# First tile's output projection: four row blocks per PSUM chain instead of two, with its weights and half of its operands in other buffer rings

## The chip, the core and the metric

The kernel runs on one core of one Trainium2 chip. The metric is the time of one execution on the device in microseconds (us); lower is better. The engines are TensorE (PE; its weight loads are PEld), VectorE (DVE), ScalarE (ACT), GpSimd (POOL) and the queues that issue transfers, SyncE's (SP) above all. Each engine executes its own instructions in the order in which the built program has them, and waits on semaphores for the others.

## What is computed

One decoder layer over 2048 tokens of width 1024, in float32. Attention and a convolution branch are put side by side and go through one output projection; a SwiGLU network follows. Cut to what the change touches:

```python
hn = rms_norm(h, mix_pre_g)
proj = hn @ w_in                                     # A
attn_out = sliding_window_attention(q, k, v, ...)    # B, 512 columns
conv_out = conformer_conv(u, ...)                    # C, 512 columns; @ w_conv_pw at its end
mixed = jnp.concatenate([attn_out, conv_out], axis=-1) @ w_out   # W: 1024 x 1024
h = h + rms_norm(mixed, mix_post_g)                  # W's tail
hn = rms_norm(h, ffn_pre_g)
ff = (jax.nn.silu(hn @ w_gate) * (hn @ w_up)) @ w_down           # F and G
```

## The kernel before

**Tiles and stages.** The 2048 tokens are four tiles of 512. A letter and a tile number name a stage; the names in the profile carry the letter (`mm@W` is a PSUM bank written by W). A is the input projection, B attention in four blocks of 128 tokens, C the convolution with its normalization, U a product of `w_conv_pw` and half of `w_out` made once (`fold`), W the output projection, H the operands of the feed-forward part, F and G that part. A matrix operand is split in two parts (high by ScalarE, the rest by VectorE), and each product of two split operands is three matmuls of 128x512.

**W, the output projection.** Per tile it sums eight input row blocks of 128 (four from attention, four from the convolution) into four 128x1024 accumulators, `acc`, in SBUF (tag `x` for tile 0). `stage_w` goes through the row blocks in groups of `G`; for a group and a half n of the output columns it loads and splits `G` weight tiles (`weights`) and calls `block_half`: for each of the four accumulators one PSUM chain of 3 x `G` matmuls, which is then copied to `acc` by ScalarE (first group) or added to it by VectorE (the others). `acts` loads the `G` operand blocks from `mixT` by way of `wx` and splits them. For tile 0, `htags` has four entries, so `G` is 2.

**Buffers.** `t_` takes a buffer of a ring by its tag; a request waits until one is free, and requests for one tag are served in the order of the program's priorities:

```python
BUFS = dict(x=4, p=4, wx=1, gb=2, hl=8, ql=4, chl=5, mid=4, mb=2, fa=4, at=2, fc=3, glu=2, yt=1, raw=2, w=6)
mm = lambda: bank("mm", 4)
```
`raw` holds weights as they come from memory, two tiles in one buffer, for A and for W alike; `w` holds split weights, before also for both. The one `yt` buffer holds the convolution's tile (`turns[t]`, made in `stage_taps`) from the first finished channel block until `conv_tail` has normalized it and written it to `mixT`. One of the two `mb` buffers holds attention's bias. `chl` is free during the last A stage.

**Order.** The main program runs the stages A0 to A3 with `run`; the others are generators in lanes that are advanced by what the main one yields, and each `yield` says how much work was laid down. `lw` holds W0; it may start when A3 has begun, conv tile 0 is done and U is done, and W0 is finished by `lw.until("W0")` before W1. A scheduler then fixes the order of every engine from these priorities and from what each instruction waits for. The taps of the convolution (lane `lc`) have a lower priority and are tied to the pace of the products. So A3, W0, attention B2, the taps of conv tiles 1 and 2 and the tail of conv tile 1 share the engines at the same time, about 330 to 440 us into the span.

Of the kernel before, what the change touches and what calls it, by code (L numbers as in the profile page):

```python
# [13 lines left out]
F32R = mybir.dt.float32r  # L14
# [11 lines left out]
P = 128  # L26
T = 512
# [10 lines left out]
def layer_kernel(ctx, tc, x, xT, cols, rows, sinks, relb, onehot, w_in, w_pw, w_out, w_gate, w_up, w_down, out):  # L38
# [10 lines left out]
    def nm(s):  # L49
        uid[0] += 1  # L50
        return f"{s}@{lab[0]}_{uid[0]}"
# [3 lines left out]
    def t_(tag, shape, dt=F32):  # L55
        return sb.tile(list(shape), dt, tag=tag, name=nm(tag), bufs=BUFS[tag])

    def f4(tag, shape=(P, D)):
        return t_(tag, shape)
# [4 lines left out]
    def hl(tag):  # L64
        return t_(tag, (P, 2, T), F32R)
# [5 lines left out]
    def bank(tag, bufs):  # L71
        return ps.tile([P, T], F32, tag=tag, name=nm(tag), bufs=bufs)

    mm = lambda: bank("mm", 4)
# [7 lines left out]
    made = {"rows": [], "at": 0, "new": True}  # L82
# [40 lines left out]
    def split_w(raw, tag, low=None, made=False, on_pool=True):  # L123
        w = tag if not isinstance(tag, str) else hl(tag)
        if made:
            nc.sync.dma_start(w[:, 1].bitcast(F32), low)
        act(w[:, 0], raw, AF.Copy)  # L127
        if not made:
            (ptt if on_pool else vtt)(w[:, 1], raw, w[:, 0].bitcast(F32), ALU.subtract)
            if low is not None:  # L130
                nc.sync.dma_start(low, w[:, 1].bitcast(F32))
        return w

    def weight(src, low, made, raw=None, on_pool=True):
        if raw is None:
            raw = t_("raw", (P, 2, T))
            nc.sync.dma_start(raw, src)
        return [split_w(raw[:, n], "w", low[n], made, on_pool) for n in range(2)]

    def kweight(u, made, raw=None):  # L140
        hs = weight(w_in[u].rearrange("p (a b) -> p a b", a=2), lo_in[u], made, raw, u < TAPS0)
# [49 lines left out]
    def three(o, pairs, first=True, last=True):  # L191
        n = 3 * len(pairs)
        i = 0
        for (sh, sl), (mh, ml) in pairs:
            for a, b in ((sh, mh), (sh, ml), (sl, mh)):
                mat(o, a, b, start=first and i == 0, stop=last and i == n - 1)
                i += 1

    lo_in = dr.tile([2 * KC - 2, 2, P, T], F32, name="lo_in")
    lo_out = dr.tile([2, KC // 2, P, T], F32, name="lo_out")  # L200
# [54 lines left out]
    started = set()  # L255
# [461 lines left out]
    def ss(s):  # L717
        return slice((s % 4) * P, (s % 4 + 1) * P)

    def block_half(acc, units, n, first, L, bank_of, s0=0):  # L720
        cs = slice(n * T, (n + 1) * T)
        for i in range(len(acc)):
            s = i + s0
            lab[0] = L
            o = bank_of()
            three(o, [((a[s // 4][:, 0, ss(s)], a[s // 4][:, 1, ss(s)]), (w[:, 0], w[:, 1])) for a, w in units])
            if first:
                act(acc[i][:, cs], o, AF.Copy)
            else:
                vtt(acc[i][:, cs], acc[i][:, cs], o, ALU.add)  # L730
            yield 0.65 * len(units)

    def stage_w(w, atag, htags, rtags, bank_of, norm=None, ready=None):
        G = KC // len(htags)
        L = f"W{w}"
        lab[0] = L
        acc = [f4(atag) for _ in range(4)]

        def acts(gi):
            aa = []  # L740
            lab[0] = L
            n = 4 if rtags[gi] == "yt" else 2
            for c in range(G * gi, G * gi + G, n):
                ms = t_(rtags[gi][c // 2 % 2] if isinstance(rtags[gi], tuple) else rtags[gi], (P, n, T))
                nc.sync.dma_start(ms, mixT[c : c + n, :, w * T : (w + 1) * T].rearrange("c p t -> p c t"))
                for j in range(n):
                    a = hl(htags[gi])
                    act(a[:, 0], ms[:, j], AF.Copy)
                    vtt(a[:, 1], ms[:, j], a[:, 0].bitcast(F32), ALU.subtract)
                    aa.append([a])  # L750
            return aa

        def weights(gi, n):
            ws = []
            for c in range(G * gi, G * gi + G, 2):
                if c < 4:
                    ws += weight(w_out[c : c + 2, :, n * T : (n + 1) * T].rearrange("c p t -> p c t"), lo_out[n, c : c + 2], w > 0, on_pool=False)
                else:
                    for j in range(2):
                        ws.append(hl("w"))  # L760
                        nc.sync.dma_start(ws[-1].bitcast(F32), fold[n, c - 4 + j])
            return ws

        nxt = acts(0)
        yield W_LEAD
        for gi in range(KC // G):
            aa = nxt
            for n in range(2):
                lab[0] = L
                if n == 1 and gi + 1 < KC // G and not (ready and G * gi + G == 4):  # L770
                    nxt = acts(gi + 1)
                ws = weights(gi, n)
                yield from block_half(acc, list(zip(aa, ws)), n, gi == 0, L, bank_of)
            if ready and G * gi + G == 4:
                for i, c in enumerate(ready()):
                    if i == Q0 // 2:
                        ld.until("C1")
                        lh.until("B21.0")
                        lab[0] = L
                        nxt = acts(gi + 1)  # L780
                    yield c
        tail = norm_w(w, acc)
        if norm:
            norm(tail)
        else:
            yield from tail

    def norm_w(w, acc):
        L = f"W{w}"
        lab[0] = L  # L790

        def whole(src):
            t = f4("chl")
            nc.sync.dma_start(t, src)
            return t

        gb = whole(rows[0].partition_broadcast(P))
        ssq = sm(4)
        for s in range(4):
            act(junk, acc[s], AF.Square, accum_out=ssq[:, s : s + 1])  # L800
            yield 0.75
            lab[0] = L
        r = rsqrt(ssq, 4, D, w < 3)
        xs = [whole(x[w * T + s * P : w * T + (s + 1) * P]) for s in range(4)]
        ssq2 = sm(4)
        yield 3
        for s in range(4):
            lab[0] = L
            stt(acc[s], acc[s], r[:, s : s + 1], gb, ALU.mult, ALU.mult)
            yield 1.25  # L810
            lab[0] = L
            vtt(acc[s], xs[s], acc[s], ALU.add)
            r0 = w * T + s * P
            nc.sync.dma_start(h_scr[r0 : r0 + P], acc[s])
            act(junk, acc[s], AF.Square, accum_out=ssq2[:, s : s + 1])
            yield 1.25
        lab[0] = L
        r2 = rsqrt(ssq2, 4, D, w < 3)
        yield 3
        for s in range(4):  # L820
            lab[0] = L
            act(xs[s], acc[s], AF.Copy, scale=r2[:, s : s + 1])
            yield 1.25
        if w == 0:
            normed.extend(xs)
        elif w == 2:
            for k in range(KC):
                u = turn_row(w, xs, k, f2("gb"))
                nc.scalar.dma_start(hT[1][k], u)
                yield 2.0  # L830
        else:
            for k in range(4):
                t = t_("mid", (P, 2, T))
                for j in range(2):
                    turn_row(w, xs, k + 4 * j, t[:, j])
                    yield 2.0
                normed.append(t)
# [540 lines left out]
    W_LEAD = 4.0  # L1378
# [12 lines left out]
    lw = Lane(RW0, 0)  # L1391
# [3 lines left out]
    lu = Lane(0.6, 0)  # L1395
    ld = Lane(2.0, 0)
# [16 lines left out]

    lb.add("X", stage_x(), lambda: "x1" in started)
    lu.add("U", stage_fold(), lambda: "A2" in started)
    lw.add("W0", stage_w(0, "x", ["hl"] * 4, ["wx"] * 4, mm), lambda: "A3" in started and "C0" in ld.done and "U" in lu.done)
    TGA = [["hl"] * 8, ["mid"] * 4 + ["chl"] * 4, ["hl"] * 8, ["mid"] * 4 + ["hl"] * 4]
    xa = {}
    warm = mm()
# [45 lines left out]
    ws, ops = (0, 1), {}  # L1465
    for n, off in (("B11", 0), ("B21", 4)):
        lh.add(n + ".0", stage_h_plain(ws, ops, n, off))
    run(stage_w(1, "mid", ["hl", "chl"], [("wx", "mb"), "yt"], mm, norm=lambda g: lh.add("N1", g), ready=lambda: stage_pre(ws, ops, mids[0], keeps[0], 0, Q0)))
    lc.hold = lambda: "S0" not in lh.done
    lh.until("B21.0")  # L1470
# [9 lines left out]
    ws, ops = (2, 3), {}  # L1480
    lw.add("C2", stage_tail(2))
    lw.add("W2", stage_w(2, "mid", ["ql", "chl"], ["chl", "yt"], tr))
    lw.add("C3", stage_tail(3), lambda: since(lc, "T3", CS))
    lw.add("W3", stage_w(3, "mid", ["ql", "chl"], ["chl", "yt"], tr, norm=lambda g: lw.add("N3", g)))
# [73 lines left out]
```

## Time and profile before

| | |
|---|---|
| median of 3 runs | 1941.39 us (1934.53 to 1942.58) |
| profiled execution | 1939.15 us |
| its span, first to last instruction | 1937.4 us |
| granted TensorE clock, mean | 0.996 |
| busy, share of the span | PE 98%, PEld 79%, DVE 76%, ACT 50%, POOL 16% |

In the profile's rows `out<-in` names what an instruction writes and reads, x and a number is a count of instructions, then busy us and mean ns; a bracket shows how long the engine had been idle before the row, and what ended that. A row by stretches gives busy us and count for PE, PEld, DVE, ACT and POOL, then the granted clock, the share of the transfer engines and GB/s; engines with nothing in the stretch are left out. In the times of a run in order (timeline), the first number is the start, the second the duration of the merged row.

### The profile page before, as it was taken

To read this page: it belongs to the slowest core of one execution; us is meant where nothing else is said; L and a number is where in the kernel's file an instruction comes from. 1 tells how busy PE (TensorE), PEld (TensorE's weight loads), DVE (VectorE), ACT (ScalarE), POOL (GpSimd) and SP (SyncE) were. 2 spreads that over 40 slices of the span, in tenths; PEclk is the share of its full clock that TensorE was granted. 3 is DMA by queue.
4 is the path that set the end of the run, shared out by engine and by line. 5 is a ranking of instruction groups with operands and counts; after the bars stand their busy time and mean duration, and the time that the engine had idled before them with its cause. 6 is when DMAs were issued, how large, how long until landed. Compare 5 with 4: busy or idle time off the path is not lost.

```text
span 1937.4 us, 26679 instructions
## 1 busy us (share of the span) xinstructions
PE 1897.0 (98%) x8730; PEld 1532.9 (79%) x8730; DVE 1475.7 (76%) x2648; ACT 959.2 (50%) x1886; POOL 310.2 (16%) x451
## 2 busy tenths in 40 slices
PE   8999999999999999999999999999999999999997
PEld 6777777677777888787888788888788888888886
DVE  4999979995986997888669964678777766455557
ACT  5365465446748533333454555567534333345453
POOL 4010121011120011211000110002033333211003
PEclk9999999999999999999999999999999999999998
DMA  8787766657758667777577875769745443375663
GB/s 306 244 307 232 229 200 237 212 192 226 255 190 308 232 231 259 250 262 239 172 256 245 305 270 196 247 232 361 262 153 167 153 147 114 115 262 187 201 202 138
DMA packets 208556, 435.68 MB, mean 225 GB/s; under 512 B 21753, under 2 KB 39329, under 8 KB 208417
## 3 DMA queue, kind: packets, MB, share of 16 engines
q1 hardware_dynamic: 188192, 394.13, 60.8%
q0 software_dynamic: 9472, 31.46, 4.7%
q10 hardware_dynamic: 10752, 8.39, 1.3%
q8 instruction: 68, 1.11, 0.2%
q14 instruction: 72, 0.58, 0.1%
HBM read 323.26 MB, written 110.63 MB: 224 GB/s over the span
## 4 chain that ended last, share of the span: by engine, by line
PE 66%; DVE 15%; DMA 12%; issue 3%; ACT 2%; POOL 2%; SPq 0%; DVEq 0%; ACTq 0%; POOLq 0%
PE mm@F L85 30%; PE mm@G L85 17%; PE mm@A L85 8%; DVE fc@C L94 5%; PE mm@W L85 4%; PE tr@W L85 3%; PE tr@B L85 2%; DMA mids<-fa@F 2%; DMA chl@H<-hT 1%; DMA fc@G<-w_down 1%; DMA raw@A<-w_in 1%; DVE w@F L94 1%; DVE fa@F L94 1%; DVE chl@F L94 1%; DMA mixT<-yt@C 1%
## 5 line engine op out<-in xcount | busy, mean ns | idle before, releaser
L94 DVE SCALAR_TENSOR_TENSOR fc@C<-glu@C,colt,fc@C 128x512 f32<-128x512 f32 x480 | 361.2, 768 | 2.7
L85 PE MATMUL mm@F<-hl@H,w@F 128*128 128x512 f32 x1056 | 256.8, 393 | 7.2 <-ACT w@F L850 4.0
L85 PEld LDWEIGHTS mm@F<-hl@H,w@F 128*128 128x128 f32 x1056 | 198.0, 189 | 52.6 <-ACT w@F L850 5.3
L85 PE MATMUL mm@G<-hl@G,hl@G 128*128 128x512 f32 x924 | 227.5, 393 | 2.2 <-DVE hl@G L94 2.2
L850 ACT ACTIVATE w@F<-chl@F 128x512 fp32r<-128x512 f32 x220 | 135.7, 626 | 175.9 <-PE mm@F L85 144.6
L85 PE MATMUL mm@A<-hl@A,w@A 128*128 128x512 f32 x840 | 209.2, 397 | 5.1 <-ACT w@A L127 2.8
L85 PEld LDWEIGHTS mm@G<-hl@G,hl@G 128*128 128x128 f32 x924 | 171.5, 188 | 38.9 <-DVE hl@G L94 3.3
L85 PE MATMUL mm@G<-w@G,hl@G 128*128 128x512 f32 x876 | 199.4, 389 | 0.0
L85 PEld LDWEIGHTS mm@A<-hl@A,w@A 128*128 128x128 f32 x840 | 156.1, 189 | 44.7 <-issue 3.9
L85 PEld LDWEIGHTS mm@G<-w@G,hl@G 128*128 128x128 f32 x876 | 164.4, 188 | 34.1
L94 DVE TENSOR_TENSOR w@F<-chl@F,w@F 128x512 fp32r<-128x512 f32 x198 | 152.9, 777 | 46.2 <-ACT w@F L850 46.0
L85 PE MATMUL mm@F<-mid@H,w@F 128*128 128x512 f32 x528 | 132.1, 390 | 1.0 <-DVE fa@F L94 0.5
L85 PE MATMUL mm@F<-ql@H,w@F 128*128 128x512 f32 x528 | 130.0, 390 | 0.0
L85 PE MATMUL mm@F<-p@H,w@F 128*128 128x512 f32 x528 | 129.1, 389 | 0.0
L85 PE MATMUL mm@F<-x@H,w@F 128*128 128x512 f32 x528 | 125.9, 391 | 0.0
L85 PEld LDWEIGHTS mm@F<-mid@H,w@F 128*128 128x128 f32 x528 | 99.0, 188 | 22.3 <-DVE fa@F L94 1.0
L85 PEld LDWEIGHTS mm@F<-x@H,w@F 128*128 128x128 f32 x528 | 98.7, 188 | 21.3 <-issue 0.8
L85 PEld LDWEIGHTS mm@F<-p@H,w@F 128*128 128x128 f32 x528 | 99.1, 188 | 20.6
L85 PEld LDWEIGHTS mm@F<-ql@H,w@F 128*128 128x128 f32 x528 | 98.8, 188 | 20.2
L516 POOL TENSOR_SCALAR_AFFINE_SELECT p@B<-p@B 128x512 f32<-128x512 f32 x62 | 56.1, 911 | 339.6 <-ACT p@B L514 338.0
L127 ACT ACTIVATE w@A<-raw@A 128x512 fp32r<-128x512 f32 x110 | 67.4, 626 | 85.5 <-PE mm@A L85 53.2
L94 DVE TENSOR_TENSOR w@G<-raw@G,w@G 128x512 fp32r<-128x512 f32 x73 | 53.4, 731 | 71.4 <-ACT w@G L850 70.5
(320 smaller groups left out, 3253.3 us busy)
## 6 DMA issues: line engine op xcount, KB each, us to landing
mids<-fa@F SPq DMA_DIRECT2D x154, 256.0 KB, 2.9
raw@A<-w_in SPq DMA_DIRECT2D x55, 512.0 KB, 4.6
w@A<-lo_in SPq DMA_DIRECT2D x84, 256.0 KB, 3.7
fc@G<-mids SPq DMA_DIRECT2D x77, 256.0 KB, 3.3
fa@G<-mids SPq DMA_DIRECT2D x75, 256.0 KB, 4.5
w@W<-fold SPq DMA_DIRECT2D x32, 512.0 KB, 5.7
gb@F<-keeps SPq DMA_DIRECT2D x54, 256.0 KB, 3.9
chl@F<-w_gate SPq DMA_DIRECT2D x22, 512.0 KB, 5.1
```

Source lines behind the costliest of these rows:

```text
L85: r = nc.tensor.matmul(*args, **kw)
L94: r = op(*args, **kw)
L127: act(w[:, 0], raw, AF.Copy)
L516: cut = nc.gpsimd.affine_select(out=pg[:, kb].rearrange("p (i q) -> p i q", q=P), in_=pg[:, 1].rearrange("p (i q) -> p i q", q=P), compare ...
L850: act(w[:, 0], x, AF.Copy)
```

## The change

It concerns W of tile 0 alone. Its eight row blocks are taken in two groups of four, not four of two. A chain then has 12 matmuls on four row blocks, and each accumulator half is evicted twice and not four times: 8 copies by ScalarE as before, 8 additions by VectorE and not 24. Its weight tiles come from ring `chl`, not `w`. The four operands of the second group come from `yt` (one buffer for two), `mb` and `chl`. And W0 yields `W_LEAD` (4.0) ahead of each `block_half`.

```diff
-    def weight(src, low, made, raw=None, on_pool=True):
+    def weight(src, low, made, raw=None, on_pool=True, tag="w"):
...
-        return [split_w(raw[:, n], "w", low[n], made, on_pool) for n in range(2)]
+        return [split_w(raw[:, n], tag, low[n], made, on_pool) for n in range(2)]
...
-    def stage_w(w, atag, htags, rtags, bank_of, norm=None, ready=None):
+    def stage_w(w, atag, htags, rtags, bank_of, norm=None, ready=None, wtag="w"):
...
+        spare = []
+
+        def room(tag, i):
+            tag = tag if isinstance(tag, str) else tag[i]
+            if tag != "yt":
+                return hl(tag)
+            if not spare:
+                spare.append(t_("yt", (P, 2, 2, T), F32R))
+            return spare[0][:, i % 2]
...
-                    a = hl(htags[gi])
+                    a = room(htags[gi], len(aa))
...
-                    ws += weight(w_out[...], lo_out[n, c : c + 2], w > 0, on_pool=False)
+                    ws += weight(w_out[...], lo_out[n, c : c + 2], w > 0, on_pool=False, tag=wtag)
...
-                        ws.append(hl("w"))
+                        ws.append(hl(wtag))
...
+                if w == 0:
+                    yield W_LEAD
                 yield from block_half(acc, list(zip(aa, ws)), n, gi == 0, L, bank_of)
...
-    lw.add("W0", stage_w(0, "x", ["hl"] * 4, ["wx"] * 4, mm), lambda: ...)
+    lw.add("W0", stage_w(0, "x", ["hl", ["yt", "yt", "mb", "chl"]], [("wx", "wx")] * 2, mm, wtag="chl"), lambda: ...)
```

What the built program makes of it, at three places. First TensorE, ahead of the sixth product bank of A3 (`mm@A_624`). Before, these rows stand there (`tr@B_588` is a transpose in attention B2's second block):

```order
L85 MATMUL mm@W_620_3874<-w@W_616_3846,hl@W_593_3706 128x512
L85 MATMUL mm@W_617_3850<-w@W_615_3842,hl@W_592_3703 128x512 x2
L85 MATMUL mm@W_617_3850<-w@W_616_3846,hl@W_593_3706 128x512 x3
L513 MATMUL tr@B_588_3674<-ident,p@B_527_3353 128x128 x4
L85 MATMUL mm@A_624_3890<-mid@A_500_3193,w@A_622_3884 128x512 x3
```
Now these (`tr@B_689` is the last bank of B2's last block, `ct@C_576` to `ct@C_582` are the transposes at the end of conv tile 1):

```order
L513 MATMUL tr@B_686_4288<-ident,p@B_655_4090 128x128 x4
L513 MATMUL tr@B_688_4298<-ident,p@B_655_4090 128x128 x4
L85 MATMUL tr@B_689_4306<-p@B_687_4297,vtok 64x512
L85 MATMUL tr@B_689_4306<-p@B_685_4287,vtok 64x512
L85 MATMUL tr@B_689_4306<-p@B_687_4297,vtok 64x512
L85 MATMUL tr@B_689_4306<-p@B_685_4287,vtok 64x512
L640 MATMUL ct@C_576_3589<-ident,yt@C_359_2283 128x128 x4
L640 MATMUL ct@C_578_3599<-ident,yt@C_359_2283 128x128 x4
L640 MATMUL ct@C_580_3609<-ident,yt@C_359_2283 128x128 x4
L640 MATMUL ct@C_582_3619<-ident,yt@C_359_2283 128x128 x4
L85 MATMUL mm@A_624_3875<-mid@A_500_3193,w@A_622_3869 128x512 x3
```
Between the last matmul of W0's fourth chain and `mm@A_624` there are now 89 rows, all of them of attention B2 and conv tile 1: all that was left of both. Before, A3's and W0's products lay among them.

Second, VectorE: after the change the rows behind the normalization of conv tile 1 (`yt@C_359`) are W0's operands and the four weight tiles of its second block half:

```order
L94 SCALAR_TENSOR_TENSOR yt@C_359_2283<-fc@C_583_3624,yt@C_359_2283 128x4x128
L94 TENSOR_TENSOR yt@W_611_3834<-wx@W_610_3832,yt@W_611_3834 128x512 x2
L94 TENSOR_TENSOR mb@W_613_3841<-wx@W_612_3839,mb@W_613_3841 128x512
L94 TENSOR_TENSOR chl@W_614_3844<-wx@W_612_3839,chl@W_614_3844 128x512
L94 TENSOR_TENSOR chl@W_616_3849<-raw@W_615_3847,chl@W_616_3849 128x512
L94 TENSOR_TENSOR chl@W_617_3853<-raw@W_615_3847,chl@W_617_3853 128x512
L94 TENSOR_TENSOR chl@W_619_3859<-raw@W_618_3857,chl@W_619_3859 128x512
L94 TENSOR_TENSOR chl@W_620_3863<-raw@W_618_3857,chl@W_620_3863 128x512
```
Before, the splits of W0's third and fourth weight tile stood among the taps of conv tile 1, some 200 rows ahead of that point.

Third, SyncE's queue, which loads A3's sixth weights (`raw@A_621`). Before:

```order
L137 DMA raw@W_614_3840<-w_out 128x2x512
L745 DMA mb@W_762_4732<-mixT 128x2x512
L126 DMA w@A_601_3745<-lo_in 128x512
L126 DMA w@A_602_3748<-lo_in 128x512
L569 DMA glu@C_468_2961<-glu_scr 128x542
L137 DMA raw@A_621_3882<-w_in 128x1024
```
Now (`raw@W_615` and `raw@W_618` were issued some 15 rows earlier):

```order
L647 DMA mixT<-yt@C_359_2283 128x4x128 x4
L755 DMA wx@W_612_3839<-mixT 128x2x512
L755 DMA wx@W_742_4691<-mixT 128x2x512
L131 DMA lo_out<-chl@W_616_3849 128x512
L137 DMA raw@A_621_3867<-w_in 128x1024
```
The load of A3's weights has moved behind the four writes of conv tile 1, the activations of W0's second group and the split of W0's next weights, whose buffer it takes.

More of the change, by code (lines that the diff above doesn't have):

```diff
@@ L756, in weights @@
                 if c < 4:
-                    ws += weight(w_out[c : c + 2, :, n * T : (n + 1) * T].rearrange("c p t -> p c t"), lo_out[n, c : c + 2], w > 0, on_pool=False)
+                    ws += weight(w_out[c : c + 2, :, n * T : (n + 1) * T].rearrange("c p t -> p c t"), lo_out[n, c : c + 2], w > 0, on_pool=False, tag=wtag)
                 else:
                     for j in range(2):
-                        ws.append(hl("w"))
+                        ws.append(hl(wtag))
                         nc.sync.dma_start(ws[-1].bitcast(F32), fold[n, c - 4 + j])
@@ L1415, in layer_kernel @@
     lu.add("U", stage_fold(), lambda: "A2" in started)
-    lw.add("W0", stage_w(0, "x", ["hl"] * 4, ["wx"] * 4, mm), lambda: "A3" in started and "C0" in ld.done and "U" in lu.done)
+    lw.add("W0", stage_w(0, "x", ["hl", ["yt", "yt", "mb", "chl"]], [("wx", "wx")] * 2, mm, wtag="chl"), lambda: "A3" in started and "C0" in ld.done and "U" in lu.done)
     TGA = [["hl"] * 8, ["mid"] * 4 + ["chl"] * 4, ["hl"] * 8, ["mid"] * 4 + ["hl"] * 4]
```

## The prediction

> **What bounds the kernel now.** I read the page first, then the busy time by stretches around the first projection (label W), then the matmul row in order of time there, then VectorE's groups in the same stretch.
>
> ```profile
> PE 1897.0 (98%) x8730; PEld 1532.9 (79%) x8730; DVE 1475.7 (76%) x2648; ACT 959.2 (50%) x1886; POOL 310.2 (16%) x451
> ```
> ```profile
> 350.00:400.00 50.00, 46.16 (x238) 35.38 (x237) 49.09 (x119) 19.34 (x60) 5.01 (x6) 1.00 0.62 202
> 400.00:450.00 50.00, 50.00 (x244) 38.38 (x243) 43.03 (x97) 25.69 (x66) 12.52 (x36) 1.00 0.65 203
> ...
> 1400.00:1500.00 100.00, 100.00 (x443) 82.81 (x442) 70.79 (x85) 38.99 (x69) 32.90 (x21) 1.00 0.50 158
> ```
> TensorE is the bound: 98% over the span, and 443 products in 100 us where nothing disturbs it, 0.226 us each. So a change pays only by taking TensorE's gaps, and costs whatever new gap it makes. Between 350 and 400 us TensorE lacks 3.84 us, while VectorE is busy 49.09 of 50: that is the place of W's additions.
>
> ```profile
> 361.71 0.97 PE L85 MATMUL tr@B<-kz,ql@A 64*128 64x256 f32 x12
> ...
> 369.28 3.06 PE L85 MATMUL mm@A<-mid@A,w@A 128*128 128x512 f32 x12 [0.94 <-DVE x@W L94]
> ...
> 386.01 1.66 PE L85 MATMUL mm@W<-w@W,hl@W 128*128 128x512 f32 x6 [2.50 <-DVE x@W L94]
> ```
> ```profile
> L94 DVE SCALAR_TENSOR_TENSOR fc@C<-glu@C,colt,fc@C 128x512 f32<-128x512 f32 x84 | 62.0, 768 | 0.1
> L94 DVE TENSOR_TENSOR x@W<-x@W,mm@W 128x512 f32<-128x512 f32 x24 | 15.7, 679 | 0.0
> L474 DVE CUSTOM_DVE_ANT_0 p@B<-tr@B,mb@X 128x128 f32<-128x128 f32 x32 | 7.5, 282 | 0.0
> L471 DVE COPY_PREDICATED tr@B<-upper,tr@B 128x256 f32<-128x256 int8 x16 | 6.2, 423 | 0.0
> L94 DVE TENSOR_TENSOR hl@W<-wx@W,hl@W 128x512 fp32r<-128x512 f32 x8 | 5.4, 685 | 0.0
> L94 DVE TENSOR_TENSOR p@B<-p@B,sm@B 128x512 f32<-128x512 f32 x8 | 5.2, 686 | 0.0
> L94 DVE TENSOR_TENSOR sm@B<-sm@B,sm@B 128x8 f32<-128x8 f32 x4 | 0.7, 163 | 0.0
> L628 DVE BATCH_NORM_STATS2 sm@C<-yt@C 128x6 f32<-128x512 f32 x4 | 2.5, 673 | 0.0
> ```
> Two waits of TensorE, 0.94 and 2.50 us, end with W's additions (x@W). The groups (330 to 440 us) show what VectorE does there: conv taps (fc@C), attention (tr@B, p@B) and 24 additions.
>
> **What goes.** With four row blocks per chain 16 of the 24 additions disappear: 16 x 15.7/24 = 10.5 us of VectorE, beside TensorE's work. On the path it is worth at most the two waits, 3.4 us. The products, the splits of weights and operands, and W's transfers keep their number. The pause that W now makes ahead of each group moves its products later in TensorE's queue; A3's products stand in their place, so that alone costs nothing.
>
> **What the rings do.** This is the term that decides. The first round's four weight tiles take four of chl's five buffers. The second half's operands need the one buffer of yt, and that holds conv tile 1 (yt@C) until its norm has been written out. The order shows the result: the raw weights of W's next round are loaded early into both buffers of raw; their splits stand on ScalarE and VectorE behind the yt operands; and those stand behind the last step of conv tile 1. Projection A of the last tile needs raw too, so its next product, the sixth bank of A3, stands behind everything that is left of attention B2 and of conv tile 1's tail. TensorE executes in this order, so it stops. I sum the way from the point where it runs dry.
>
> TensorE runs dry after the scores at 361.71 + 0.97 = 362.7, less 7 products that the order has not yet there (1.6): 361.1.
>
> VectorE up to the statistics of conv tile 1. The changed order has two VectorE instructions fewer ahead of the row at 363.25 below (1.2 us), so I start at 363.25 - 1.2 + 0.6 = 362.65.
>
> ```profile
> 342.82 5.51 DVE L94 SCALAR_TENSOR_TENSOR fc@C<-glu@C,colt,fc@C 128x512 f32<-128x512 f32 x8
> ...
> 363.25 0.69 DVE L94 SCALAR_TENSOR_TENSOR fa@A<-fa@A,mm@A 128x512 f32<-128x512 f32 x1
> ```
> From there the order has 49 taps, one tap start, 10 masks, 20 score reductions, 4 halves of p. A tap in a row takes 5.51/8 = 0.69 with its overhang, so 0.68: 33.3, and 0.5 for the start. Masks 10 x 6.2/16 = 3.9; reductions 20 x 7.5/32 = 4.7; p 4 x 5.2/8 = 2.6; a dozen 8-wide ones, 0.7/4 each with overhang and about 0.1 without, 1.1. Sum 46.1; ends overlap a little (eight taps took 5.51, not 8 x 0.768), so 45. Then 362.65 + 45 = 407.7. VectorE next waits for four of eight exponentials and the copy of the last conv block on ScalarE:
>
> ```profile
> L495 ACT ACTIVATE p@B<-p@B,sm@B 128x128 f32<-128x128 f32 x32 | 12.4, 390 | 10.5 <-DVE sm@B L94 10.5
> L127 ACT ACTIVATE w@A<-raw@A 128x512 fp32r<-128x512 f32 x17 | 10.7, 627 | 22.0 <-PE mm@A L85 18.7 <-issue 2.5 <-PE mm@W L85 0.5
> ```
> 4 x 0.39, and about 0.6 for the copy (a split of the same size takes 10.7/17), 2.1: 409.8. The tail behind it is a chain with no other work to fill it:
>
> ```profile
> 441.37 0.20 POOL L153 TENSOR_TENSOR sm@C<-sm@C 128x4 f32<-128x4 f32 x1
> ...
> 447.48 0.20 POOL L156 TENSOR_TENSOR sm@C<-sm@C,sm@C 128x4 f32<-128x4 f32 x1
> ...
> 464.69 0.20 POOL L153 TENSOR_TENSOR sm@W<-sm@W 128x4 f32<-128x4 f32 x1 [17.02 <-DVE sm@W L94]
> ...
> 467.77 0.20 POOL L156 TENSOR_TENSOR sm@W<-sm@W,sm@W 128x4 f32<-128x4 f32 x1
> ```
> ```profile
> 451.35 2.93 ACT L636 ACTIVATE yt@C<-yt@C,sm@C,sm@C 128x512 f32<-128x512 f32 x4 [1.80 <-DVE sm@C L94]
> 478.63 0.60 PE L640 MATMUL ct@C<-ident,yt@C 128*128 128x128 f32 x4
> ...
> 479.95 0.77 ACT L645 ACTIVATE yt@C<-ct@C,lnh 128x512 f32<-128x512 f32 x1
> 480.75 0.69 DVE L94 SCALAR_TENSOR_TENSOR yt@C<-fc@C,yt@C 128x512 f32<-128x512 f32 x1 [2.85 <-ACT yt@C L645]
> ```
> ```profile
> raw@A<-w_in SPq DMA_DIRECT2D x12, 512.0 KB, 5.1
> wx@W<-mixT SPq DMA_DIRECT2D x4, 512.0 KB, 4.1
> mixT<-yt@C SPq DMA_DIRECT2D x4, 256.0 KB, 3.2
> ```
> - statistics 2.5, p 1.2, small ones 1: 4.7
> - the root on GpSimd: 3.3 alone (464.69 to 467.97), 6.3 among other work (441.37 to 447.68); 5.5, since the four selects of B2's last block lie between
> - the scaling 0.3 + 2.93: 3.2
> - four blocks through ct's only bank, each from the transposes at 478.63 to 479.95 + 0.77: 2.1 x 4, and the last product 0.7: 9.1
> - writing conv out frees yt: 0.4 + 3.2 = 3.6
> - two operands split, two copies at 0.6 and one subtraction: 1.9
> - the next activations into the one wx buffer: 0.4 + 4.1 = 4.5
> - four splits on ScalarE (mb, chl, and the two weights of the first raw buffer), 2.2, and VectorE's last 0.7: 2.9
> - A's raw weights 0.3 + 5.1 = 5.4, their split 0.63: 6.0
>
> Sum 41.4, so TensorE goes on at 451.2, 90.1 us after it ran dry. Not all is lost: what it does of B2 and conv in between is gone later.
>
> ```profile
> 362.60:453.20 90.60, 16.75 (x114) 8.84 (x112) 8.62 (x30) 6.41 (x11) 1.00 0.64 207
> ```
> ```profile
> 428.00:480.00 52.00, 3.48 (x20) 2.56 (x20) 5.63 (x9) 1.00 0.78 249
> ```
> These are tr@B and ct@C alone, 16.75 + 3.48 = 20.2 busy; up to 0.2 us at the end of each of some 25 runs of them lies under the next product, so it is 15 to 20, and I take 18. Net 72.1.
>
> **The restart.** After a wait of 3.14 us before's own trace shows a slower clock:
>
> ```profile
> 1370.00:1380.00 10.00, 10.00 (x36) 7.65 (x37) 7.85 (x14) 5.22 (x10) 0.00 (x0) 0.83 0.76 253
> ```
> ```profile
> 1369.87 13.03 PE L85 MATMUL mm@F<-hl@H,w@F 128*128 128x512 f32 x48 [3.14 <-ACT w@F L850]
> ```
> 48 products took 13.03 instead of 48 x 0.226 = 10.9: 2.1 us. I add 2.1, once. The Trainium skill, page "TensorE: Matmul & The Clock Gate", Part 1, says that a long idle stretch brings the array to half rate and about 3.4 us of sustained work bring it back; half rate for that long would lose an estimated 1.7 us, and by it the sum would be 0.4 us lower; the trace's 2.1 agrees with it that far. The same rule speaks against this change in a second way: the scattered transposes of the stop would run at half rate too, which no row of before shows.
>
> **The sum.** 72.1 + 2.1 - 3.4 = 70.8. The profiled execution took 1939.15 us (span 1937.4 and 1.75 around it), 2.2 below the median of the three runs, within their spread. 1939.15 + 70.8 = 2010.
>
> The bounds. Low: root at 3.3, all 20.2 us credited, no exponentials waited for, no slow clock, transposes of the next block overlapped (-2), landings 1 us shorter each: -2.2 - 2.2 - 2.1 - 2.1 - 2 - 3 = -13.6, 1996. High: landings 1.5 longer each, only 15 credited, VectorE waiting in attention for 6: 4.5 + 3 + 6 = 13.5, 2023, and a second stop. W's tail (its norm) ends later against the other work:
>
> ```profile
> 432.94 0.63 DVE L94 TENSOR_TENSOR x@W<-x@W,mm@W 128x512 f32<-128x512 f32 x1
> ```
> ```profile
> 468.43 4.27 ACT L822 ACTIVATE chl@W<-x@W,sm@W 128x1024 f32<-128x1024 f32 x4
> ```
> From the last addition to the first normed block it took 433.6 to 469.5, 36 us, among conv tile 1's work. The order leaves about 140 products, 32 us, between W's last product and the transposes of that block. Conv is done by then, so I count nothing; at the old length it would be 4 us more.
>
> **Rivals.**
> 1. Attention sets the pace, not VectorE's work. Its exponentials came 48.7 us apart over two blocks:
> ```profile
> 377.31 0.40 ACT L495 ACTIVATE p@B<-p@B,sm@B 128x128 f32<-128x128 f32 x1 [3.98 <-DVE sm@B L94]
> ...
> 425.99 0.39 ACT L495 ACTIVATE p@B<-p@B,sm@B 128x128 f32<-128x128 f32 x1
> ```
> Then the last block's come at 425.99 again instead of about 408: +18, 2028. For it: nothing shows a faster round. Against it: in those rounds B waited behind products and additions that are absent in the stop. 0.10.
> 2. Conv tile 1's tail is as slow as before. From
> ```profile
> 432.24 0.68 DVE L628 BATCH_NORM_STATS2 sm@C<-yt@C 128x6 f32<-128x512 f32 x1
> ```
> to 480.75 + 0.69 it took 49.2, against 22.5 in my chain: +27, 2037. Against it: its transposes stood there behind products of A and W. 0.05.
> 3. There is no stop. If yt were free before TensorE has used up what is loaded, only the 3.4 us of waits would go: 1936, not slower. It decides at about 361 us; before's own trace has conv tile 1 in yt until 481. 0.04.
>
> **Numbers.** My forecast, 2010, has 0.81. The range 1996 to 2032 takes in its bounds and rival 1; rival 2 and 3 lie outside. About 0.5% (9.7 us) is what a measurement of this kernel can tell from no change. Rival 3 alone is not slower: faster by more 0.01, within 0.03, slower 0.96.
>
> **What would show it.** The changed kernel's trace should have a stretch of some 90 us from about 361 in which the matmul row holds only tr@B and ct@C, ended by mm@A waiting for ScalarE's w@A; raw@W loaded before it and split in its last 10 us; yt@W right behind the last yt@C; VectorE idle in its second half; 8 additions x@W. If mm@A runs on through 361 to 450, the forecast is wrong at its root; if the stop is there but its first part is over 60 us, attention set it, if its second part is over 50, the tail did.

## The result and the profile after

| | median, us | lowest to highest |
|---|---|---|
| before | 1938.81 | 1934.53 to 1942.58 |
| changed | 2009.56 | 2005.60 to 2011.36 |

The changed kernel takes 1.0363 times as long (95% interval 1.034 to 1.0386). Its profiled execution took 2005.6 us, span 2003.9, the fastest of its four runs.

From the page, the busy line and the clock by slices:

```profile
PE 1912.3 (95%) x8730; PEld 1542.3 (77%) x8730; DVE 1464.8 (73%) x2632; ACT 959.5 (48%) x1886; POOL 319.4 (16%) x451
PE   8999999539999999999999999999899999999997
PEclk9999999759999999999999999999999999999998
```
One hole in TensorE's row, in slices 8 and 9 (350 to 450 us), where the granted clock falls too. VectorE has 16 instructions fewer, 2632 for 2648. The stretches (TensorE, weight load, VectorE, ScalarE, GpSimd, then granted clock, DMA share, GB/s):

```profile
350.00:400.00 50.00, 25.78 (x143) 16.34 (x142) 50.00 (x125) 15.86 (x62) 7.41 (x8) 0.72 0.12 32
400.00:450.00 50.00, 15.24 (x50) 6.57 (x49) 24.36 (x55) 21.03 (x46) 8.40 (x20) 0.57 0.29 89
450.00:500.00 50.00, 50.00 (x212) 41.20 (x213) 7.50 (x11) 12.77 (x22) 1.33 (x2) 0.96 0.66 215
```
First VectorE is full and everything else waits for it; then no engine is full, DMA included: a chain. After 450 TensorE is full again. The hole in the matmul row, first and last rows with some between:

```profile
357.68 0.95 PE L85 MATMUL mm@W<-chl@W,hl@W 128*128 128x512 f32 x3
358.56 0.98 PE L85 MATMUL tr@B<-kz,ql@A 64*128 64x256 f32 x12
...
379.10 1.65 PE L85 MATMUL tr@B<-kz,ql@A 64*128 64x256 f32 x12 [9.79 <-DVE sm@B L474]
...
426.11 1.12 PE L640 MATMUL ct@C<-ident,yt@C 128*128 128x128 f32 x4 [1.54 <-ACT yt@C L645]
428.76 1.11 PE L640 MATMUL ct@C<-ident,yt@C 128*128 128x128 f32 x4 [1.54 <-ACT yt@C L645]
449.91 4.96 PE L85 MATMUL mm@A<-mid@A,w@A 128*128 128x512 f32 x12 [20.03 <-ACT w@A L127]
454.71 1.75 PE L85 MATMUL mm@W<-chl@W,hl@W 128*128 128x512 f32 x7
456.30 2.88 PE L85 MATMUL mm@A<-hl@A,w@A 128*128 128x512 f32 x12
```
From the end of the scores at 359.5 to 449.9, 90.4 us, TensorE does only B2's and conv tile 1's small products, and is let go by the split of A's weights. Why that split is late is read on the queue of loads and on ScalarE:

```profile
327.08 0.43 SPq L137 DMA_DIRECT2D raw@W<-w_out  x1
329.50 0.38 SPq L137 DMA_DIRECT2D raw@W<-w_out  x1
443.63 0.34 SPq L137 DMA_DIRECT2D raw@A<-w_in  x1
```
```profile
434.68 1.15 ACT L758 ACTIVATE yt@W<-wx@W 128x512 fp32r<-128x512 f32 x2 [3.31 <-DMA mixT<-yt@C]
440.44 0.63 ACT L758 ACTIVATE mb@W<-wx@W 128x512 fp32r<-128x512 f32 x1 [4.62 <-DMA wx@W<-mixT]
440.98 0.61 ACT L758 ACTIVATE chl@W<-wx@W 128x512 fp32r<-128x512 f32 x1
441.50 2.17 ACT L127 ACTIVATE chl@W<-raw@W 128x512 fp32r<-128x512 f32 x4
449.23 1.15 ACT L127 ACTIVATE w@A<-raw@A 128x512 fp32r<-128x512 f32 x2 [5.56 <-DMA raw@A<-w_in]
```
Raw weights asked for at 327 and 329 are split at 441.5; in between no raw weights are loaded at all. yt@W's first split waits for conv tile 1's write-out (mixT<-yt@C), as the buffer of yt does.

### The profile page after: what moved, and what is told of

The parts are those of the page before. It is cut to its first block, busy times and chain, and to the rows that moved or that the text cites. A ratio compares the mean times of both kernels' runs of the same rounds, so it can differ in the third digit from the quotient of the medians.

```text
span 2003.9 us, 26651 instructions
## 1 busy us (share of the span) xinstructions
PE 1912.3 (95%) x8730; PEld 1542.3 (77%) x8730; DVE 1464.8 (73%) x2632; ACT 959.5 (48%) x1886; POOL 319.4 (16%) x451
## 3 DMA queue, kind: packets, MB, share of 16 engines
q8 instruction: 68, 1.11, 0.2%
## 4 chain that ended last, share of the span: by engine, by line
PE 64%; DVE 18%; DMA 9%; issue 4%; ACT 3%; POOL 2%; SPq 0%; DVEq 0%; ACTq 0%; POOLq 0%
PE mm@F L85 32%; PE mm@G L85 16%; PE mm@A L85 8%; DVE fc@C L94 8%; PE mm@W L85 3%; PE tr@W L85 2%; PE tr@B L85 1%; DMA raw@A<-w_in 1%; DMA raw@F<-w_gate 1%; DVE hl@G L94 1%; DVE mid@W L94 1%; DVE w@F L94 1%; DMA mids<-fa@F 1%; DVE p@B L474 1%; DMA keeps<-fa@F 1%
## 5 line engine op out<-in xcount | busy, mean ns | idle before, releaser
L85 PEld LDWEIGHTS mm@F<-ql@H,w@F 128*128 128x128 f32 x528 | 98.8, 188 | 20.2
L85 PE MATMUL mm@A<-mid@A,w@A 128*128 128x512 f32 x336 | 92.0, 402 | 20.0 <-ACT w@A L127 20.0
```

Of the source, the lines that this page charges most:

```text
L85: r = nc.tensor.matmul(*args, **kw)
```

## The experiments

Each edit is a difference to the changed kernel unless said otherwise; its arguments are those of the line that adds W0. "All hl" means that no operand lies in yt, mb or chl.

### What makes the stop: yt, and which links carry it

**No operand in the free buffers** (e4_all_hl):
```diff
-["hl", ["yt", "yt", "mb", "chl"]]
+["hl", "hl"]
```


> The changed kernel with all operands from hl: chains of four, weights in chl and the pause stay, no operand in yt, mb or chl. Theory: yt's hold was the root, so there is no stop; TensorE runs through 361 to 450, 16 additions fewer are worth at most the two waits of 3.4 us: 1934 to 1942, within 0.5% of the kernel before. Rival (chains of four need four operands and four weights at once, and the operands now press on ring hl, or weights in chl delay work on chl elsewhere): a new wait near 350 to 450, 1948 or more.

Measured 1943.41 us against 1938.18 (ratio 1.0029, interval 1.0017 to 1.0042). The 90 us are gone; chains of four, weights in chl and the pause do not make them. But the forecast gain is not there, and some 5 us are lost. The stretch says where, TensorE at 43.96 us and a clock of 0.90:

```profile
350.00:400.00 50.00, 43.96 (x215) 33.57 (x214) 48.45 (x112) 23.38 (x64) 4.65 (x6) 0.90 0.55 180
```
That is taken up below with the pause. The profiled execution was the fastest of the ten (1939.01): counted by the k-th matmul (its start in this trace less its start in the trace of before), it falls back by 8.0 us from matmul 1600 to 1800 and is level again at the end, so the 5 us between the medians do not show in it as a whole.

**Only yt undone** (e14_mb_only), against the next run a difference of yt alone:
```diff
-["hl", ["yt", "yt", "mb", "chl"]]
+["hl", ["hl", "hl", "mb", "hl"]]
```


> The changed kernel with its second half's operands in hl, hl, mb, hl: against the run with yt, yt, mb, hl only yt is taken out. Theory (yt is the root of the long stop, mb is free in time): no long stop, only the 6 us wait around 360 that the pause makes: 1939 to 1947. Rival (mb holds the second half too): over 1952.

Measured 1947.64 (1.0041, 1.0025 to 1.0057): no long stop, so the root is yt. It lies 0.6 us above what was expected. One wait in its trace is new, of W's tail, the place that the prediction priced at 4 us if it slipped:

```profile
495.02 0.34 PE L857 MATMUL ct@H<-ident,chl@W 128*128 128x128 f32 x1 [2.35 <-ACT chl@W L834]
```
More goes there than the wait itself: by the k-th matmul this trace, of the slowest of the five executions, falls back against before by 8.3 us from matmul 2200 to 2400, that of the run with all operands from hl by 3.9.

**The fourth operand from hl** (e1_fourth_hl), so that the next weights need not stand behind it for chl:
```diff
-["hl", ["yt", "yt", "mb", "chl"]]
+["hl", ["yt", "yt", "mb", "hl"]]
```


> The changed kernel with one word altered: W's fourth operand of the second half from ring hl, so that ring chl holds weights only. Theory (a chain of buffers: the weights of W's next round fill both buffers of raw, and their splits stand behind operands that need yt and chl): the weights get chl's fifth buffer without standing behind the fourth operand, raw comes free, and A3 goes on by about 176 products (some 40 us) beyond 361. A second link remains: W's second half still needs yt, so TensorE then stops at about 400 until conv tile 1 is written out and the yt operand is split, about 437 to 447. Loss 40 to 47 us, less some 10 for the small products done in it, plus 2 for the slower clock: 1963 to 1980, likeliest 1971. Rival 1 (the wait for yt alone makes the whole stop, whatever raw does): still 2004 to 2014, dry from 360. Rival 2 (the chain through chl and raw makes all of it): no stop, 1934 to 1942.

Measured 1970.56 (1.0169, 1.0145 to 1.0192). The stop begins at 402.2, 43 us later, and is ended by another releaser:

```profile
404.30 0.66 PE L578 MATMUL ct@C<-ident,fc@C 128*128 128x128 f32 x4 [2.08 <-DVE fc@C L94]
...
441.75 2.38 PE L85 MATMUL mm@W<-chl@W,yt@W 128*128 128x512 f32 x6 [3.09 <-ACT yt@W L758]
```
So the stop has two links, both from yt: A3's raw weights, held through W's weights, and W's own second half. Both rivals fall: neither alone makes it.

**The same link cut by order** (e2_weights_first):
```diff
-                if n == 1 and gi + 1 < KC // G and not (ready and G * gi + G == 4):
+                ahead = n == 1 and gi + 1 < KC // G and not (ready and G * gi + G == 4)
+                if ahead and w:
                     nxt = acts(gi + 1)
                 ws = weights(gi, n)
+                if ahead and not w:
+                    nxt = acts(gi + 1)
```

> The changed kernel with the order of two requests swapped: in W0 the second round's weights are asked for ahead of the next four operands; all rings as in the change. Theory: the weights' splits no longer stand behind the yt operands, so raw comes free and the first link is cut as in the run with the fourth operand from hl; the wait for yt is left, with a stop from about 400 to about 440: 1963 to 1980, within 8 us of that other run, though it reaches this by another edit. Rival 1 (yt alone): 2004 to 2014. Rival 2 (raw's link is all): 1934 to 1942.

Measured 1978.52 (1.0215, 1.0196 to 1.0235), 8 us above the last run: at the edge of "within 8". Its stop ends 7.9 us later, with another wait:

```profile
449.67 4.18 PE L85 MATMUL mm@W<-chl@W,yt@W 128*128 128x512 f32 x9 [7.79 <-DMA chl@W<-fold]
```
The fourth operand needs chl here again, and the folded weights of the second half are asked for behind it; that this is the 8 us was not tried.

**Weights back in ring w** (e11_yt_four_w), operands as in the change:
```diff
-wtag="chl"
+wtag="w"
```


> The changed kernel with W0's weights from ring w instead of chl; operands in yt, mb and chl as in the change. Theory (two links: chl and raw stop A3's sixth bank, yt alone stops W's second half): with no weights in chl the first link is gone and only the second is left, TensorE dry from about 400 until the yt operands are split near 440 to 447: 1960 to 1985, as with the fourth operand from hl. Rival (the hold of raw needs no chl, the yt operands alone keep raw from A): 2000 to 2014.

Measured 1966.44 (1.0143, 1.013 to 1.0156): as the theory had it. The waits:

```profile
368.36 4.21 PE L85 MATMUL mm@A<-mid@A,w@A 128*128 128x512 f32 x9 [5.69 <-ACT w@A L127]
...
440.61 2.93 PE L85 MATMUL mm@W<-w@W,yt@W 128*128 128x512 f32 x6 [5.44 <-ACT yt@W L758]
```

**yt alone** (e9_yt_twos), the kernel before with two operands in yt:
```diff
-["hl"] * 4
+["hl", "hl", ["yt", "yt"], "hl"]
```


> The kernel before with one thing of the change: the two operands of W's third group come from yt; groups of two, weights from w, no pause. Theory (the hold of yt by conv tile 1 is the root, whatever the chains' length): in the order A3's seventh bank now stands behind 92 small products of B2 and conv tile 1, beginning some 24 us later than in the changed kernel, at about 384, and ending when the yt operands are split, about 437 to 447. 53 to 63 us, less some 13 for the small products, plus 2: 1978 to 1992. Rival (it takes chains of four or weights in chl to make a stop): 1934 to 1944.

Measured 1982.68 (1.0234, 1.0216 to 1.0251). Groups of two, weights from w, no pause, and still a stop of 63 us:

```profile
376.40 4.79 PE L85 MATMUL mm@W<-w@W,hl@W 128*128 128x512 f32 x19
385.62 1.65 PE L85 MATMUL tr@B<-kz,ql@A 64*128 64x256 f32 x12 [4.44 <-DVE sm@B L474]
...
444.17 1.22 PE L85 MATMUL mm@W<-w@W,yt@W 128*128 128x512 f32 x2 [5.48 <-ACT yt@W L758]
445.18 4.23 PE L85 MATMUL mm@A<-mid@A,w@A 128*128 128x512 f32 x12
```
```profile
378.21 0.33 SPq L137 DMA_DIRECT2D raw@A<-w_in  x1
```
raw is not held here, since A's loads go on to 378; W's products on yt simply stand ahead of A3's seventh bank in TensorE's order. One buffer whose holder leaves late (yt@W is first split at 443.5 here) is enough, by whichever link.

### The pause, and where the small gain is

**No pause** (e3_no_pause):
```diff
-                if w == 0:
-                    yield W_LEAD
```


> The changed kernel without the added pause of W0 ahead of each group (yield W_LEAD). Theory: the pause has nothing to do with the stop, which comes from buffers; the same stretch without products from about 360, 85 to 92 us long, and 2000 to 2014. Rival (the pause pushes W's products behind work that they then wait for): the stop shrinks with it, 1935 to 1960.

Measured 2001.61 (1.0339, 1.0316 to 1.0362). The stop stays. Without the pause W's products stand first behind it and start 8.5 us earlier, but meet a second wait:

```profile
441.41 10.26 PE L85 MATMUL mm@W<-chl@W,hl@W 128*128 128x512 f32 x35 [12.24 <-ACT chl@W L127]
...
463.88 2.05 PE L85 MATMUL mm@W<-chl@W,yt@W 128*128 128x512 f32 x4 [3.82 <-DMA chl@W<-fold]
```
Its profiled span, 2005.1, is no shorter than the changed kernel's; its median is 8 us lower. The two were not run side by side, and their profiled runs lie at opposite ends of their spreads, so what the pause is worth inside the change stays open.

**All hl, no pause** (e7_all_hl_no_pause) and **all hl, weights from w, with the pause** (e8_four_alone):
```diff
-["hl", ["yt", "yt", "mb", "chl"]]
+["hl", "hl"]
-                if w == 0:
-                    yield W_LEAD
```


> All operands from hl, chains of four, weights in chl, without the pause ahead of each group. Theory (chl's five buffers hold back the second round's splits, and with them raw): the pause is beside the point, the wait of some 6 us around 360 stays, 1940 to 1946. Rival (the pause orders W's requests so that raw is held): without it the wait is gone and the additions' gain shows, 1932 to 1938.

```diff
-["hl", ["yt", "yt", "mb", "chl"]], wtag="chl"
+["hl", "hl"], wtag="w"
```


> Chains of four and the pause alone: all operands from hl, weights from ring w as before. Theory (chl's size holds raw): w is the ring that A's weights use in turn, so W's second round waits for its w buffers together with its raw loads; no 6 us wait for w@A around 360, and the 16 additions less are worth up to 3.4 us: 1932 to 1940. Rival 1 (chains of four with both raw buffers asked for at once hold raw whatever ring the splits go to): the wait stays, 1940 to 1948. Rival 2 (W's four weights crowd A's out of ring w): longer waits of A3 for w, over 1948.

Measured 1934.46 (0.9975, 0.9965 to 0.9986) without the pause, and 1942.39 (1.0025, 1.0014 to 1.0035) with it and weights in w. My theory fell twice: chl's size is not the cause, the pause is. The splits of W's second round and A's next raw load, weights in chl, first with the pause (one row of ScalarE, one of the queue), then without it:

```profile
355.82 2.00 ACT L127 ACTIVATE chl@W<-raw@W 128x512 fp32r<-128x512 f32 x3
```
```profile
361.20 0.33 SPq L137 DMA_DIRECT2D raw@A<-w_in  x1
```
```profile
350.70 0.64 ACT L127 ACTIVATE chl@W<-raw@W 128x512 fp32r<-128x512 f32 x1 [2.09 <-PE mm@W L85]
```
```profile
351.63 0.33 SPq L137 DMA_DIRECT2D raw@A<-w_in  x1
```
The splits need the weight buffers of the first round, which its products let go. The pause makes those later, raw stays full meanwhile, and A's load comes 9.6 us later. The waits that follow, first with weights in chl, then in w, both with the pause:

```profile
360.20 1.01 PE L85 MATMUL tr@B<-kz,ql@A 64*128 64x256 f32 x12 [1.93 <-DVE sm@B L474]
363.76 1.11 PE L513 MATMUL tr@B<-ident,p@B 128*128 128x128 f32 x4 [2.54 <-DVE p@B L94]
365.78 5.49 PE L85 MATMUL mm@A<-mid@A,w@A 128*128 128x512 f32 x12 [0.91 <-ACT w@A L127]
```
```profile
367.31 5.06 PE L85 MATMUL mm@A<-mid@A,w@A 128*128 128x512 f32 x11 [5.73 <-ACT w@A L127]
```
In the first, two waits for attention stand ahead of the 0.91, where no product of A was ready.

**Chains of four alone** (e10_four_w_no_pause), and **the pause alone** on the kernel before (e13_twos_hl_pause):
```diff
-["hl", ["yt", "yt", "mb", "chl"]], wtag="chl"
+["hl", "hl"], wtag="w"
-                if w == 0:
-                    yield W_LEAD
```


> Chains of four alone: operands from hl, weights from ring w as before, no pause. Theory after the last runs (the pause makes the first round's products end late, so the second round's splits wait for weight buffers while their raw loads already hold both buffers of raw, and A3's raw load comes some 8 us late): without the pause no wait for w@A around 360, 1931 to 1938, like the run with weights in chl and no pause. Rival (weights in ring w crowd A's, pause or not): the wait for w@A stays, 1940 to 1948.

```diff
                 ws = weights(gi, n)
+                if w == 0:
+                    yield W_LEAD
```


> The kernel before with the pause alone: groups of two, operands from hl, weights from ring w. Theory (the pause costs only where a round asks for both buffers of raw at once): a round of two weights asks for one raw buffer, A3 keeps the other, so the pause costs nothing measurable: 1934 to 1943. Rival (the pause itself delays W and TensorE with it): 1944 to 1952.

Measured 1932.37 (0.9966, 0.9954 to 0.9979) and 1933.25 (0.9974, 0.9965 to 0.9983). Both beat the kernel before by their intervals, and the first is the best of all; against the run with weights in w and the pause it is 10 us faster. So the pause costs 9 to 10 us (differences of medians) in chains of four, where a round asks for both raw buffers, and nothing in chains of two, where it asks for one. That fits the hold of raw; what else differs between the two lengths was not separated. The additions in the two, in that order:

```profile
L94 DVE TENSOR_TENSOR x@W<-x@W,mm@W 128x512 f32<-128x512 f32 x8 | 5.2, 677 | 0.4 <-PE mm@W L85 0.4
```
```profile
L94 DVE TENSOR_TENSOR x@W<-x@W,mm@W 128x512 f32<-128x512 f32 x24 | 15.7, 679 | 4.4 <-PE mm@W L85 4.4
```
With 24 additions or 8 the gain is the same within the intervals. TensorE's waits of 2.50 and 0.94 us for x@W are 0.41 in the second:

```profile
358.47 0.63 PE L578 MATMUL ct@C<-ident,fc@C 128*128 128x128 f32 x4 [1.44 <-DVE fc@C L94]
389.43 3.02 PE L85 MATMUL mm@A<-mid@A,w@A 128*128 128x512 f32 x12 [0.41 <-DVE x@W L94]
```
So these two waits shrink by when W runs, too; that fewer additions bring anything by themselves was not shown. Nor do the traces show that the gain comes from the two waits. TensorE's idle time from 350 to 500 us is 3.84 us before, 3.91 with chains of four alone, 3.98 with all hl and no pause and 3.05 with the pause alone: other waits have come in their place. With chains of four alone the largest is (in total, times, longest):
```profile
PE tr@B L85 <- POOL p@B L516: 3.4, 2, 2.2
```
By the k-th matmul chains of four alone are 1.8 us ahead of before at matmul 1600, where W0's products begin, 0.7 ahead at 2800, behind W0, and 3.6 at the end; the pause alone is 2.0, 1.4 and 5.7 ahead. So in these traces, of one execution each, the gain is not made in W0's stretch, and where it comes from stays open. (Chains of four alone were profiled in an execution 3 us above their median.)

**Weights in chl alone** (e6_chl_two), on the kernel before:
```diff
-["hl"] * 4, ["wx"] * 4, mm
+["hl"] * 4, ["wx"] * 4, mm, wtag="chl"
```


> The kernel before, groups of two row blocks, operands from hl, with one thing of the change: W0's weights come from ring chl. It tells apart where the 6 us went that TensorE waited around 358 to 366 in the run with all operands from hl. Theory: there, a round of four weights fills four of chl's five buffers, the next round's raw weights are already loaded into both buffers of raw, and three of their four splits wait for chl until the first round's products are done (raw loaded at 326 and 329, split at 355.8), so A3's raw load comes late. With two weights a round chl has room for two rounds, raw is let go at once, no such wait: 1932 to 1942, the same as before. Rival (chl is busy with the conv and norm steps and W's weights wait there whatever their number): A3 waits for its split again, 1942 or more.

Measured 1942.06 (1.0017, 1.0005 to 1.0028). No wait for w@A around 360, as the theory has it; but the time is at the rival's edge. Counted by the k-th matmul of both traces it is 2.3 us ahead of before at matmul 2700 and 4.4 behind at 3100, in stage F, far behind W0. TensorE waits 7.0 us there (560 to 660 us) against 2.0 before: for copies of F's banks 3.5 against 1.7, for W's normed blocks in chl 2.0 against 0.3, for attention's p 1.5 against none. What moved them I did not find.

## Why the prediction was right

**Bound and place.** Forecast: dry at 361.1, going on at 451.2, 90.1 us. Measured 359.5, 449.9, 90.4. That yt is the root, and that the first link runs over chl and raw, is shown by e14 and by e1 and e11. The prediction named one link only; the second (W's own chains) lay hidden behind it, and alone left the time 28 to 32 us above before (e11, e1), the short wait around 360 included.

**The first part** was forecast at 45 us of VectorE's work and a wait of 2.1; it ran from 360.65 to 408.37, 47.7 us, of which 46.3 were work and 1.4 a wait. The first row below begins 0.65 us earlier, so it has 46.96 busy:

```profile
360.00:408.37 48.37, 20.09 (x97) 10.70 (x97) 46.96 (x117) 13.28 (x52) 11.21 (x12) 0.63 0.08 23
408.37:449.91 41.54, 10.97 (x38) 4.45 (x34) 17.40 (x35) 17.58 (x35) 4.60 (x16) 0.58 0.31 99
```
Rival 1 (attention sets the pace) is out: the last block's exponentials do not come at 425.99 again, and VectorE lacks 1.4 us, not 18:

```profile
406.21 0.40 ACT L495 ACTIVATE p@B<-p@B,sm@B 128x128 f32<-128x128 f32 x1 [3.52 <-DVE sm@B L94]
```

**The tail**, forecast 41.4, took 41.54. Its joints on VectorE:

```profile
408.37 0.69 DVE L628 BATCH_NORM_STATS2 sm@C<-yt@C 128x6 f32<-128x512 f32 x1 [1.41 <-ACT yt@C L579]
...
418.41 0.16 DVE L94 SCALAR_TENSOR_TENSOR sm@C<-sm@C,sm@C 128x4 f32<-128x4 f32 x1 [5.38 <-POOL sm@C L156]
...
431.40 0.69 DVE L94 SCALAR_TENSOR_TENSOR yt@C<-fc@C,yt@C 128x512 f32<-128x512 f32 x1 [1.96 <-ACT yt@C L645]
435.34 1.29 DVE L94 TENSOR_TENSOR yt@W<-wx@W,yt@W 128x512 fp32r<-128x512 f32 x2 [3.25 <-ACT yt@W L758]
441.11 0.69 DVE L94 TENSOR_TENSOR mb@W<-wx@W,mb@W 128x512 fp32r<-128x512 f32 x1 [4.47 <-ACT mb@W L758]
442.32 2.49 DVE L94 TENSOR_TENSOR chl@W<-raw@W,chl@W 128x512 fp32r<-128x512 f32 x4
```
| link | forecast | measured |
|---|---|---|
| statistics and root | 4.7 + 5.5 | 4.7 + 5.4 |
| scaling | 3.2 | 3.1 |
| four blocks through ct | 9.1 | 10.55 |
| writing out | 3.6 | 2.6 |
| yt operands, next wx | 1.9 + 4.5 | 1.95 + 3.8 |
| splits | 2.9 | 3.2 |
| A's raw and its split | 6.0 | 6.3 |

The blocks through ct took 1.45 us more, the two transfers ahead of the splits 1.0 and 0.7 less: the misses cancel. The blocks were slower because their transposes took 1.11 us for four, against 0.60 in before's row: the slow clock, which the prediction named for them but charged at the restart only. Rival 2 is out: from the first statistics to the last yt@C it took 23.7 us, not 49. Rival 3 (no stop) is out too.

**Credit and restart.** The restart was forecast at 2.1: the first 12 and 7 products after 449.91 took 6.39 us, 19 x 0.226 = 4.29, so 2.1. Counted by the k-th matmul of both traces, the changed kernel is 1.6 us ahead at matmul 1700 and 68.3 behind at 2400, 69.9 lost in between, where the forecast's terms make 70.8. From this the credit can be worked out: 90.4 + 2.1, less 3.4 for the two waits, less 69.9 leaves an estimated 19 us of what TensorE did in the stop, where the forecast took 18 of 15 to 20.2. (At the slow clock these products were busy for 20.09 + 10.97 = 31 us.)

**The gain of 3.4** came, but its reason is not shown. In the changed kernel the two waits are gone: between the stop and matmul 2400 TensorE waits 0.3 us in all. That 16 additions fewer bring this is not shown: with all 24 and the pause the two waits shrink as well (e13), and where the additions are fewer and there is no stop, other waits take their place (e10, e7).

**The step that does not stand** is the pause, which "alone costs nothing". With chains of four it costs 9 to 10 us once the stop is gone (e4 against e7, e8 against e10), as it leaves raw full for longer; A3's products, which were to stand in W's place, then have no weights. What it costs inside the stop stays open (e3).

**The sum.** 70.8 forecast; 66.5 between the two profiled spans, 70.75 between the medians. That the forecast meets the median within 0.5 us is partly luck: the changed kernel's profiled run was 4 us below its median.

**W's tail** was counted at nothing, and no wait for it over 0.3 us stands in the changed kernel's trace.

## What to carry to other kernels

A buffer that is free in its share of time is not free when it is asked for: before moving a tile to another ring, find in the trace when the present holder leaves it (here 435 us, needed by 360), and follow what stands behind the request on every queue, the shared staging buffers above all. A change made of four parts is judged part by part: chains of four alone were 0.34% faster, yt alone 2.3% slower. And a small gain needs its place in the trace before it gets a cause: in the trace at hand the 0.34% did not lie where the additions went. A pause is priced by what is held while it lasts, not by the engine that it leaves free.

## What the runs showed of the hardware

TensorE stayed slow while conv tile 1's transposes went, though it was never idle for long there: four of them took 1.11 us with waits of only 1.54 us between the groups, and the granted clock was 0.50:

```profile
423.40:429.87 6.47, 3.34 (x12) 2.15 (x12) 2.08 (x3) 2.89 (x5) 0.00 (x0) 0.50 0.35 105
```
The prediction drew on the Trainium skill, page "TensorE: Matmul & The Clock Gate", Part 1, which says that a long idle stretch halves the rate and sustained work of about 3.4 us restores it. The trace agrees on the half rate: the granted clock was 0.50 from 429.87 to 449.91 too, and 0.67 over the 6.39 us behind the stop, so that an estimated 4.2 us of work went at half rate. Work in bursts of about 1 us out of 2.65 did not restore it here. Even the short wait in the run with chains of four, weights in w and the pause, 5.73 us, made the next 11 products last 5.06 us, at a granted clock of 0.50, where 11 x 0.226 is 2.5.
